# Expert steps of a diffusion trunk kernel: flips at the step's own end, small products placed among whole-array ones, the first light step one place earlier

## The chip, the cores and the metric

The kernel runs on one core of one Trainium2 chip. The metric is the time of one execution on the device in microseconds; three executions give 1393.93, 1398.74 and 1399.1 us, and their median is 1398.74 us. One more execution was taken with the hardware profiler.

## The reference

A trunk of two layers over 256 latent tokens of width 1024, with 256 context tokens beside them. Layer 0 is attention and a dense SwiGLU; layer 1 is a short convolution and then a top-2-of-8 expert SwiGLU, which is the part that the change touches:

```
logits = h @ router_w
top_vals, top_idx = top_k(logits, 2); gates = one_hot(top_idx) weighted by softmax(top_vals)
out = sum over e of gates[:, e] * swiglu(h, w_gate[e], w_up[e], w_down[e])
swiglu(h, g, u, d) = (silu(h @ g) * (h @ u)) @ d
x = x + g2 * out
```

All of it is float32. An expert's hidden width is 3584; the weights of the eight experts are 352 MB, and every one is read once.

## The kernel before, in words

**Steps.** The experts are ranked by how many tokens chose them (`ranks`). Rank 0 is expert 0 of the data; ranks 1 to 4 are heavy too and take up to 128 tokens, ranks 5 to 7 are light and take up to 64. Each expert is worked through in seven steps of 512 hidden columns, so there are 35 heavy and 21 light steps; `chunks` is their order. Heavy steps of rank 0 come first, then light ones are spread evenly among the heavy ones, and the last four are light. The first light step stands at place 5, counted from 0.

**One step** is a loop over p. In p = 0 to 7 TensorE makes gate and up for this step: a heavy step in 48 products of 128x128 by 512 columns, with each weight split into a high and a low part of float32r (`parts`: ScalarE makes `hi`, L74, VectorE `lo`, L75) and the tokens split likewise (`eh`, `el`); a light step in products of plain float32 with 64 columns of weights, gate and up side by side in the array (`pair`, L1340). In p = 8 to 11 it makes the down products of the step before (`down`), again split when that step was heavy, paired when it was light. Between them lie the activations: `hidden_part` makes silu(gate) * up in the tile `sg` (ScalarE L1333, VectorE L1334), of which there is one; `flip` transposes it in four blocks on TensorE (L1320); `turned` copies it out (ScalarE L1325 or L1328, VectorE L1329). Before the change `hidden_part` of a step is issued in its p = 9, and `flip` and `turned` in p = 3 and 4 of the next step. For a light step `flip` transposes 64 rows into 64 columns.

**Tasks.** Small pieces of work hang on hooks (step, p), run at the beginning of that p. For an expert whose first step is n and whose last is `end`: `choice` (one-hot of its tokens), `slots` (its transpose and the token list, on TensorE) with `slotted` (copies), `fetch_rows` (VectorE casts the list, POOL issues an indirect DMA that gathers the rows from `xd`, a copy of x in DRAM, L1253; the rows take one slot of the weights' ring), `scale_rows` (ScalarE, L1257), `turn_rows` (transposes, L1267) with `gathered` (ScalarE L1293 builds modulated rows in a tile `sg`, L1299 casts them into `eh`, VectorE L1300 makes `el`) or `gathered_light`; at the end `output` (VectorE L1350 into a tile `sg`, ScalarE L1352, VectorE L1353), `scatter` (TensorE, L1360) and `scattered` (VectorE, L1367).

**Order.** The order on each engine is the order in which the program issues, written out by hand. Weight loads of 1 MB are issued on SP's queue as slots of a ring of 13 come free; `ahead` issues the splits up to five halves before their use, into five buffers, and for a light step's weights, which TensorE reads unsplit, only the loads. A tile of a pool may be taken anew while an older use of it is still to be issued; the new writer then waits for the last reader. PSUM gives four tiles for products and transposes (`pm`) and four for the down sums (`acc`).

The main lines of the loop are L1455 to L1492, of the hooks L1369 to L1408, of `store_rows` L1442.

Of the kernel before, what the change touches and what calls it, by code (L numbers as in the profile page):

```python
# [8 lines left out]
F32 = mybir.dt.float32  # L9
F32R = mybir.dt.float32r  # L10
I32 = mybir.dt.int32
AF = mybir.ActivationFunctionType
# [4 lines left out]
KD = D // 128  # L17
S = 256
NT = S // 128
NE = 8  # L20
# [3 lines left out]
NL = 3  # L24
CAP = 64
# [8 lines left out]
def trunk(ctx, tc, i, out, dbg=None):  # L34
    nc = tc.nc
    pe, act, dve, sp = nc.tensor, nc.scalar, nc.vector, nc.sync
    dbg = dbg or {}

    def pool(name, bufs, space=None, side="left"):
        kw = {"space": space} if space else {"side": side}  # L40
        return tc.tile_pool(name=name, bufs=bufs, reuse_waits="tile", **kw)
# [7 lines left out]
    def acc():  # L49
        return cur["acc"].tile([128, 512], F32, name="acc")  # L50

    def pm():
        return cur["pm"].tile([128, 512], F32, name="pm")
# [25 lines left out]
    order = [i["w_out"][u] for u in range(4)]  # L79
# [7 lines left out]

    heavy = [(r, c) for r in range(NE - NL) for c in range(NFC)]
    light = [(r, c) for r in range(NE - NL, NE) for c in range(NFC)]
    mixed = [((2 * n + 1) / len(v), m, rc) for m, v in enumerate((heavy[4:], light[:-4])) for n, rc in enumerate(v)]  # L90
    chunks = heavy[:4] + [rc for *_, rc in sorted(mixed)] + light[-4:]
    who, whole = {}, []

    def weights(m, r, c, h):
# [45 lines left out]
    def ahead(split):  # L140

        n = used[0]
        step = 2 if whole[n // 2] else 1
        upto, k = n, n + step
        while split and k <= most[0] and k // 2 - n // 2 < 9:
            if whole[k // 2]:
                k += 2
            else:
                upto, k, split = k, k + 1, split - 1
        feed(upto)  # L150
        used[0] += step
        return ready.pop(n)
# [4 lines left out]
    x = const.tile([128, NT, D], F32, name="x")  # L157
    ident, sel = cid[:, 0:128], cid[:, 128:130]
# [482 lines left out]
    class Pair:  # L641
# [54 lines left out]
        def turned(self):  # L696
            self.pts = [pb2.tile([128, 512], F32, name="pt") for _ in range(2)]
            for e in range(2):
                act.copy(self.pts[e], self.tp[e])
# [31 lines left out]
    for n in range(NP + 3):  # L731
# [59 lines left out]
        if new is not None and n >= new + 2:  # L791
            a = n - new - 2
# [52 lines left out]
    class Boundary:  # L845
# [11 lines left out]
        def flip(self, t, g):  # L857
            for k in range(2):
                kk = 2 * g + k
                pe.transpose(self.turn[g][:, k, t * 128:(t + 1) * 128], self.xs[:, t, kk * 128:(kk + 1) * 128], ident)  # L860
# [122 lines left out]
    for g in range(NG):  # L983
# [10 lines left out]
        sg = ph.tile([128, 512], F32, name="sg")  # L994
        hd = ph.tile([128, 512], F32, name="hd")
# [37 lines left out]
    for j in range(4):  # L1033
# [9 lines left out]
        for m, ((_, p), (_, u)) in enumerate(zip(columns(pcc), columns(pu))):  # L1043
            n = m + 1 if j == 0 else 2
# [4 lines left out]
        for m in range(2):  # L1049
            k = 2 * j + m  # L1050
# [113 lines left out]
    me = ctx.enter_context(pool("me", 2))  # L1164
    xd = ctx.enter_context(tc.tile_pool(name="xd", bufs=1, space=bass.MemoryType.DRAM)).tile([S, D], F32, name="xd")

    gts = m1.tile([128, NT, NE], F32, name="gts")
    posr = m1.tile([128, NT, NE], F32, name="posr")
# [146 lines left out]

    def flip(C):
        C.ps = pm()
        w = CAP if C.E.light else 128
        for k in range(4):
            pe.transpose(C.ps[:, k * w:(k + 1) * w], C.hd[:, k * 128:(k + 1) * 128], ident[0:w, 0:w])  # L1320

    def turned(C):
        if C.E.light:
            C.dh = me.tile([128, 4 * CAP], F32, name="dT")
            act.copy(C.dh, C.ps[:, 0:4 * CAP])  # L1325
            return
        C.dh, C.dl = (me.tile([128, 512], F32R, name=n, bufs=1) for n in ("dh", "dl"))
        act.copy(C.dh, C.ps)  # L1328
        dve.tensor_sub(C.dl, C.ps, C.dh.bitcast(F32))  # L1329

    def hidden_part(C):
        sg = me.tile([128, 512], F32, name="sg", bufs=1)[0:CAP if C.E.light else 128]
        act.activation(sg, C.g, AF.Silu)  # L1333
        dve.tensor_mul(sg, C.u, sg)  # L1334
        C.hd = sg

    def pair(ps, lhsT, ws, first, last):

        for m, w in enumerate(ws):
            pe.matmul(ps[m * CAP:(m + 1) * CAP], lhsT, w, start=first, stop=last, tile_position=(0, m * CAP))  # L1340
# [25 lines left out]
        macc = cur["macc"]  # L1366
        dve.tensor_add(macc[:, t, c], (x if E is experts[0] else macc)[:, t, c], E.ps)  # L1367

    hooks = {}  # L1369

    def hook(n, p, f, *a):
        hooks.setdefault((n, p), []).append((f, a))

    def run(n, p):
        for f, a in hooks.pop((n, p), []):
            f(*a)

    experts = [Expert() for _ in range(NE)]
    for r, E in enumerate(experts):
        E.r, E.light = r, r >= NE - NL  # L1380
        E.ys, E.eh, E.el = [None, None], [None, None], [None, None]
        steps = [n for n, (v, _) in enumerate(chunks) if v == r]
        n, end = steps[0], steps[-1]
        if r:
            hook(n - 3, 10, choice, E, posr)
            hook(n - 2, 2, slots, E)
            hook(n - 2, 3, slotted, E)
            hook(n - 2, 4, fetch_rows, E)
            hook(n - 1, 2, scale_rows, E)
            if E.light:  # L1390
                hook(n - 1, 5, turn_rows, E, range(KD))
                hook(n - 1, 6, gathered_light, E)
            else:
                for g in range(2):
                    ks = range(4 * g, 4 * g + 4)
                    hook(n - 1, (5, 8)[g], turn_rows, E, ks)
                    hook(n - 1, (6, 9)[g], gathered, E, ks)
        else:
            hook(2, 1, choice, E, pos)
            hook(2, 2, slots, E)  # L1400
            hook(2, 3, slotted, E)
        if end < len(chunks) - 1:
            for q in range(1 if E.light else 2):
                hook(end + 2, (1, 4)[q], output, E, q)
            for m in range(4):
                q, t = (m % 2, m // 2) if E.light else (m // 2, m % 2)
                hook(end + 2 + m // 2, (6, 10)[m % 2], scatter, E, q, t)
                hook(end + 2 + m // 2, (8, 11)[m % 2], scattered, E, q, t)  # L1408
    choice(experts[0], pos, True)
    most[0] = 2 * len(order) - 1  # L1410
    feed(2 * FIRST + 3)
    for g in (0, 2):
        ks = [range(2 * g, 2 * g + 2), range(2 * g + 2, 2 * g + 4)]
# [13 lines left out]
    def down(C, s):  # L1427

        E, r = C.E, C.c * 4 + s
        if r == 0:  # L1430
            E.accs = [acc() for _ in range(1 if E.light else 2)]
        first, end = r == 0, r == 4 * NFC - 1
        if E.light:
            if s % 2 == 0:
                C.w = ahead(5)
            f = [slice(s % 2 * 1024 + 512 * q, s % 2 * 1024 + 512 * q + 512) for q in range(2)]
            pair(E.accs[0], C.dh[:, s * CAP:(s + 1) * CAP], [C.w[:, v] for v in f], first, end)
        else:
            k = slice(s * 128, (s + 1) * 128)
            mac(E.accs, C.dh[:, k], C.dl[:, k], *halves(ahead(4)), first, end)  # L1440

    def store_rows():  # L1442
        for t in range(NT):
            sp.dma_start(xd[t * 128:(t + 1) * 128, :], x[:, t])

    hook(0, 1, ranks)
    hook(1, 0, store_rows)
    hook(0, 3, by_rank, posr, pos)
    hook(1, 1, gates)
    hook(3, 2, gate_rows, 1, 5, (0, 1), g2)  # L1450
# [2 lines left out]
    last, final = None, len(chunks) - 1  # L1453
    for n, (r, c) in enumerate(chunks):
        E = experts[r]  # L1455
        C = Expert()
        C.E, C.c = E, c
        if E.light:
            C.gu = pm()
            C.g, C.u = C.gu[0:CAP], C.gu[CAP:]  # L1460
        else:
            C.g, C.u = pm(), pm()
        for p in range(8):
            run(n, p)
            if last and p == 3:
                flip(last)
            if last and p == 4:
                turned(last)
            if E.light:
                if p % 4 == 0:  # L1470
                    ws = [ahead(5) for _ in range(2)]
                f = slice(p % 4 * 512, p % 4 * 512 + 512)
                pair(C.gu, E.h[:, p], [w[:, f] for w in ws], p == 0, p == 7)
                continue
            half, m, j = p // 4, (p // 2) % 2, p % 2
            hi, lo = ahead(4)
            for k in range(2):
                f = slice(k * 512, (k + 1) * 512)
                kk = 4 * half + 2 * j + k
                mac([C.u if m else C.g], E.eh[kk // 4][:, kk % 4], E.el[kk // 4][:, kk % 4], [hi[:, f]], [lo[:, f]],  # L1480
                    kk == 0, kk == KD - 1)
        for p in range(8, 12):
            run(n, p)
            if p == (8 if n in (0, final) else 9):
                hidden_part(C)
            if n == final and p == 11:
                flip(C)
                turned(C)
            if last:
                down(last, p - 8)  # L1490
        last = C
    ends = {(q, t): pm() for q in range(2) for t in range(NT)}  # L1492

    macc = cur["macc"]
# [8 lines left out]
    for t in range(NT):  # L1503
        for q in range(2):
            c = slice(512 * q, 512 * q + 512)
# [159 lines left out]
```

## Time and profile before

| what | value |
|---|---|
| median of three executions | 1398.74 us |
| the profiled execution | 1398.09 us |
| its span | 1396.2 us |
| TensorE busy | 1359.2 us, 97% |
| VectorE busy | 987.4 us, 71% |
| ScalarE busy | 798.3 us, 57% |
| read from HBM | 470.21 MB, 338 GB/s over the span |

The span is the time between the first and the last instruction that the profile shows; the execution's own time is 1.9 us longer. TensorE is called PE, VectorE DVE, ScalarE ACT, GpSimd POOL and SyncE SP. A time such as 914.28 is counted in us from the start of the span. The expert stage begins at about 503 us. A duration of a product is that of one that fills and drains the array; the distance from one start to the next is what a product costs in a row of products. Fp32 products and transposes show as one or two records each.

### The profile page before, as it was taken

The page shows a single profiled execution, that of the slowest core. Times are in us where ns is not written, and L with a number is a line of the kernel's source. Part 1 is how long each engine was busy: PE and PEld are TensorE (multiplying, and loading weights), DVE is VectorE, ACT ScalarE, POOL GpSimd, SP SyncE. Part 2 cuts the span into 40 slices and gives each one's busy share as a digit, 9 for nine tenths or more (in the row PEclk, how much of TensorE's full clock was granted, in tenths as well). Part 3 has the DMA queues.
Part 4 walks back from the last instruction along what each step waited for, and adds up shares of the span by engine and source line. Part 5 has one row for each costly group of instructions (what it writes and reads, how often), then busy time and mean ns, then how long its engine had stood idle before and what let it go on. Part 6 is the DMA issues. An engine that isn't in the chain of part 4 may idle for free.

```text
span 1396.2 us, 20283 instructions
## 1 busy us (share of the span) xinstructions
PE 1359.2 (97%) x7596; PEld 997.2 (71%) x7596; DVE 987.4 (71%) x1338; ACT 798.3 (57%) x1077; POOL 10.3 (1%) x11
## 2 busy tenths in 40 slices
PE   6999999999999999999999999999999999999997
PEld 4776789999889977766666766657667666676742
DVE  5777769788778678866767667767577677676721
ACT  5567674444463377856656666656557566565610
POOL 0000000000000000000000000000000000000000
PEclk9999999999999999999999999999999999999999
DMA  9734678678767399798999999998999999999994
GB/s 376 278 121 141 253 301 302 241 284 295 266 240 255 144 377 357 262 422 333 420 421 421 419 377 420 407 400 367 419 414 421 415 383 379 405 421 418 415 419 165
DMA packets 67162, 473.71 MB, mean 339 GB/s; under 512 B 7472, under 2 KB 8112, under 8 KB 11120
## 3 DMA queue, kind: packets, MB, share of 16 engines
q1 hardware_dynamic: 66240, 469.46, 84.2%
q0 software_dynamic: 816, 2.88, 0.6%
q8 instruction: 61, 1.00, 0.3%
q14 instruction: 45, 0.37, 0.1%
HBM read 470.21 MB, written 2.10 MB: 338 GB/s over the span
## 4 chain that ended last, share of the span: by engine, by line
PE 88%; DVE 5%; ACT 4%; DMA 2%; issue 1%; SPq 0%; ACTq 0%; DVEq 0%
PE pm L1340 11%; PE pm L274 9%; PE pm L276 8%; PE pm L278 8%; PE acc L274 8%; PE acc L276 7%; PE acc L278 7%; PE acc L1340 4%; PE pm L930 4%; PE pm L931 4%; PE pm L932 4%; PE pm L1320 2%; DVE lo L75 2%; DMA raw<-in_moe_g_dram 1%; ACT hi L74 1%
## 5 line engine op out<-in xcount | busy, mean ns | idle before, releaser
L75 DVE TENSOR_TENSOR lo<-raw,hi 128x1024 fp32r<-128x1024 f32 x522 | 627.0, 1224 | 135.8 <-ACT hi L74 113.1
L74 ACT ACTIVATE hi<-raw 128x1024 fp32r<-128x1024 f32 x522 | 546.2, 1061 | 246.0 <-PE pm L278 107.5
L274 PE MATMUL pm<-hi,eh 128*128 128x512 f32 x560 | 226.0, 404 | 0.4 <-ACT g L260 0.2
L276 PE MATMUL pm<-lo,eh 128*128 128x512 f32 x560 | 220.3, 393 | 2.1 <-DVE lo L75 2.0
L278 PE MATMUL pm<-hi,el 128*128 128x512 f32 x560 | 219.6, 392 | 0.0
L1340 PE MATMUL pm<-raw,hl 128*64 128x512 f32 x672 | 155.4, 599 | 0.0
L930 PE MATMUL pm<-th,hi 128*128 128x256 f32 x480 | 135.4, 282 | 0.0
L931 PE MATMUL pm<-tl,hi 128*128 128x256 f32 x480 | 135.0, 281 | 0.0
L932 PE MATMUL pm<-th,lo 128*128 128x256 f32 x480 | 135.0, 281 | 0.0
L274 PEld LDWEIGHTS pm<-hi,eh 128*128 128x128 f32 x560 | 105.8, 189 | 33.9 <-issue 8.0
L276 PEld LDWEIGHTS pm<-lo,eh 128*128 128x128 f32 x560 | 106.0, 189 | 24.7 <-DVE lo L75 4.5
L278 PEld LDWEIGHTS pm<-hi,el 128*128 128x128 f32 x560 | 105.8, 189 | 22.8
L1340 PEld LDWEIGHTS pm<-raw,hl 128*64 128x64 f32 x672 | 44.1, 136 | 80.6 <-issue 77.9
L930 PEld LDWEIGHTS pm<-th,hi 128*128 128x128 f32 x480 | 91.2, 190 | 1.2 <-issue 0.8
L932 PEld LDWEIGHTS pm<-th,lo 128*128 128x128 f32 x480 | 91.5, 191 | 0.0
L931 PEld LDWEIGHTS pm<-tl,hi 128*128 128x128 f32 x480 | 90.9, 189 | 0.4
L274 PE MATMUL acc<-hi,dh 128*128 128x512 f32 x280 | 88.7, 398 | 0.0
L276 PE MATMUL acc<-lo,dh 128*128 128x512 f32 x280 | 86.5, 390 | 0.0
L278 PE MATMUL acc<-hi,dl 128*128 128x512 f32 x280 | 86.3, 389 | 0.0
L1334 DVE TENSOR_TENSOR sg<-pm,sg 128x512 f32<-128x512 f32 (+1 forms) x56 | 38.6, 690 | 64.6 <-ACT sg L1333 64.3
L1340 PE MATMUL acc<-raw,dT 128*64 128x512 f32 x336 | 78.1, 600 | 0.0
L1333 ACT ACTIVATE sg<-pm 128x512 f32<-128x512 f32 (+1 forms) x56 | 32.8, 585 | 69.5 <-PE pm L1340 66.4
(329 smaller groups left out, 1613.4 us busy)
## 6 DMA issues: line engine op xcount, KB each, us to landing
raw<-in_moe_d_dram SPq DMA_DIRECT2D x112, 1024.0 KB, 12.8
raw<-in_moe_g_dram SPq DMA_DIRECT2D x111, 1024.0 KB, 13.1
raw<-in_moe_u_dram SPq DMA_DIRECT2D x111, 1024.0 KB, 12.9
raw<-in_ada_w_dram SPq DMA_DIRECT2D x48, 1024.0 KB, 6.7
raw<-in_conv_i_dram SPq DMA_DIRECT2D x12, 1024.0 KB, 7.0
raw<-in_ffn_g_dram SPq DMA_DIRECT2D x11, 1024.0 KB, 6.3
raw<-in_ffn_u_dram SPq DMA_DIRECT2D x11, 1024.0 KB, 5.7
raw<-in_ffn_d_dram SPq DMA_DIRECT2D x11, 1024.0 KB, 5.0
```

Source lines behind the costliest of these rows:

```text
L74: act.activation(hi, r, AF.Copy)
L75: dve.tensor_sub(lo, r, hi.bitcast(F32))
L274: pe.matmul(p, hh, wh[j], start=first, stop=False)
L276: pe.matmul(p, hh, wl[j], start=False, stop=False)
L278: pe.matmul(p, hl, wh[j], start=False, stop=last)
L930: pe.matmul(d, hi[:, c], th[:, k], start=(k == 0), stop=False)
L931: pe.matmul(d, hi[:, c], tl[:, k], start=False, stop=False)
L932: pe.matmul(d, lo[:, c], th[:, k], start=False, stop=(k == KD - 1))
L1320: pe.transpose(C.ps[:, k * w:(k + 1) * w], C.hd[:, k * 128:(k + 1) * 128], ident[0:w, 0:w])
L1333: act.activation(sg, C.g, AF.Silu)
L1334: dve.tensor_mul(sg, C.u, sg)
L1340: pe.matmul(ps[m * CAP:(m + 1) * CAP], lhsT, w, start=first, stop=last, tile_position=(0, m * CAP))
```

## The change

- The order of the steps: three heavy steps come first in place of four, so the first light step stands at place 4.
- `hidden_part` is issued right after p = 7 of its own step, and `flip` after p = 11 of its own step; `turned` follows in p = 1 of the next step (after the last step, at once).
- `flip` always transposes 128 rows by 128 columns; of a light step `turned` copies the 64 columns that matter.
- `slots`, `turn_rows` and `scatter` become tasks of a step, ordered by kind (turns, slots, scatters) and put at places that depend on the step: in a light step at p = 8, 9, 10, 11, in a heavy one at p = 4, 7, 9, 10, 11, each with its copies one p later. For slots the step is n - 3 (before: n - 2).
- `choice` goes to step n - 4, `fetch_rows` from p = 4 to p = 8 of step n - 2, `scale_rows` from p = 2 to p = 3 of step n - 1.
- `store_rows`, the copy of x to `xd`, goes from SP's queue to ScalarE's, and to step 0.

```diff
-    mixed = [... for m, v in enumerate((heavy[4:], light[:-4])) for n, rc in enumerate(v)]
-    chunks = heavy[:4] + [rc for *_, rc in sorted(mixed)] + light[-4:]
+    mixed = [... for m, v in enumerate((heavy[3:], light[:-4])) for n, rc in enumerate(v)]
+    chunks = heavy[:3] + [rc for *_, rc in sorted(mixed)] + light[-4:]
...
     def flip(C):
         C.ps = pm()
-        w = CAP if C.E.light else 128
         for k in range(4):
-            pe.transpose(C.ps[:, k * w:(k + 1) * w], C.hd[:, k * 128:(k + 1) * 128], ident[0:w, 0:w])
+            pe.transpose(C.ps[:, k * 128:(k + 1) * 128], C.hd[:, k * 128:(k + 1) * 128], ident)
...
-    hooks = {}
+    hooks, tasks = {}, {}
+
+    def task(n, order, *a):
+        tasks.setdefault(n, []).append((order, *a))
...
         if r:
-            hook(n - 3, 10, choice, E, posr)
-            hook(n - 2, 2, slots, E)
-            hook(n - 2, 3, slotted, E)
-            hook(n - 2, 4, fetch_rows, E)
-            hook(n - 1, 2, scale_rows, E)
+            hook(max(n - 4, 0), 10, choice, E, posr)
+            task(max(n - 3, 1), 1, [(slots, E)], [(slotted, E)])
+            hook(n - 2, 8, fetch_rows, E)
+            hook(n - 1, 3, scale_rows, E)
             if E.light:
-                hook(n - 1, 5, turn_rows, E, range(KD))
-                hook(n - 1, 6, gathered_light, E)
+                task(n - 1, 0, [(turn_rows, E, range(KD))], [(gathered_light, E)])
             else:
                 for g in range(2):
                     ks = range(4 * g, 4 * g + 4)
-                    hook(n - 1, (5, 8)[g], turn_rows, E, ks)
-                    hook(n - 1, (6, 9)[g], gathered, E, ks)
+                    task(n - 1, 0, [(turn_rows, E, ks)], [(gathered, E, ks)])
         else:
             hook(2, 1, choice, E, pos)
-            hook(2, 2, slots, E)
-            hook(2, 3, slotted, E)
+            task(2, 1, [(slots, E)], [(slotted, E)])
...
-                hook(end + 2 + m // 2, (6, 10)[m % 2], scatter, E, q, t)
-                hook(end + 2 + m // 2, (8, 11)[m % 2], scattered, E, q, t)
+                task(end + 2 + m // 2, 2, [(scatter, E, q, t)], [(scattered, E, q, t)])
+
+    for n, v in tasks.items():
+        v.sort(key=lambda a: a[0])
+        places = [(p, p + 1) for p in range(8, 12)] if chunks[n][0] >= NE - NL else [(4, 5), (7, 8), (9, 10), (10, 11), (11, 12)]
+        for (_, pe_, other), (p, q) in zip(v, places):
+            for fa in pe_:
+                hook(n, p, *fa)
+            for fa in other:
+                hook(n, q, *fa)
...
-            sp.dma_start(xd[t * 128:(t + 1) * 128, :], x[:, t])
+            act.dma_start(xd[t * 128:(t + 1) * 128, :], x[:, t])
...
-    hook(1, 0, store_rows)
+    hook(0, 2, store_rows)
...
         for p in range(8):
             run(n, p)
-            if last and p == 3:
-                flip(last)
-            if last and p == 4:
+            if last and p == 1:
                 turned(last)
...
+        hidden_part(C)
         for p in range(8, 12):
             run(n, p)
-            if p == (8 if n in (0, final) else 9):
-                hidden_part(C)
-            if n == final and p == 11:
-                flip(C)
-                turned(C)
             if last:
                 down(last, p - 8)
+        flip(C)
+        run(n, 12)
         last = C
+    turned(last)
```

## Rows read from the trace of the kernel before

**Rows 1.** The page: busy time, share of the span and instructions of each engine.

```profile
PE 1359.2 (97%) x7596; PEld 997.2 (71%) x7596; DVE 987.4 (71%) x1338; ACT 798.3 (57%) x1077; POOL 10.3 (1%) x11
```

**Rows 2.** Timeline of PE, three steps: start, us, operation, count [idle before, releaser].

```profile
914.28 0.66 PE L1320 MATMUL pm<-cid,sg 128*128 128x128 f32 x4
914.87 2.79 PE L1340 MATMUL pm<-raw,hl 128*64 128x512 f32 x12
...
930.42 0.39 PE L278 MATMUL pm<-hi,el 128*128 128x512 f32 x1
930.74 0.46 PE L1320 MATMUL pm<-cid,sg 64*128 64x64 f32 x4
931.13 0.50 PE L274 MATMUL pm<-hi,eh 128*128 128x512 f32 x1
931.47 0.39 PE L276 MATMUL pm<-lo,eh 128*128 128x512 f32 x1
...
938.16 3.65 PE L1340 MATMUL acc<-raw,dT 128*64 128x512 f32 x16
...
945.96 0.60 PE L1320 MATMUL pm<-cid,sg 128*128 128x128 f32 x4
946.32 0.48 PE L274 MATMUL pm<-hi,eh 128*128 128x512 f32 x1
946.64 0.40 PE L276 MATMUL pm<-lo,eh 128*128 128x512 f32 x1
...
953.26 0.62 PE L274 MATMUL acc<-hi,dh 128*128 128x512 f32 x2
...
958.79 1.51 PE L1340 MATMUL pm<-raw,hl 128*64 128x512 f32 x6
```

**Rows 3.** PE's gaps; a wait of DVE; two windows (PEclk third from the end).

```profile
537.62 0.43 PE L1305 MATMUL pm<-cid,oh 128*128 128x128 f32 x2 [1.62 <-DVE oh L1245]
...
719.48 0.66 PE L1320 MATMUL pm<-cid,sg 128*128 128x128 f32 x4 [1.52 <-DVE sg L1334]
...
900.04 0.47 PE L1360 MATMUL pm<-yh,ohTl 64*128 64x512 f32 x1 [1.74 <-DVE dl L1329]
...
DVE sg L1350 <- PE pm L1320: 18.3, 7, 7.4
...
538.90:542.20 3.30, 3.30 (x12) 2.62 (x11) 1.45 (x2) 1.50 (x2) 0.00 (x0) 0.50 1.01 402
717.00:720.40 3.40, 1.88 (x12) 0.70 (x10) 2.27 (x3) 1.16 (x3) 0.00 (x0) 1.00 1.01 419
```

**Rows 4.** Timeline of PE and DVE where the first expert step ends.

```profile
514.67 0.39 PE L274 MATMUL pm<-hi,eh 128*128 128x512 f32 x1
...
517.81 0.69 DVE L1334 TENSOR_TENSOR sg<-pm,sg 128x512 f32<-128x512 f32 x1
```

**Rows 5.** Groups by line from 520 us on: busy us, mean ns | idle before, releasers.

```profile
L1333 ACT ACTIVATE sg<-pm 128x512 f32<-128x512 f32 (+1 forms) x55 | 32.2, 585 | 69.4 <-PE pm L1340 66.4 <-DVE el L1300 3.0
...
L1325 ACT COPY dT<-pm 128x256 f32<-128x256 f32 x21 | 7.5, 358 | 15.6 <-PE pm L1320 15.6
...
L1257 ACT ACTIVATE raw<-raw,gs 128x1024 f32<-128x1024 f32 x4 | 4.6, 1139 | 5.4 <-DMA raw<-xd,idx 5.4
```

**Rows 6.** The gathers: one cast and its POOL issue (timeline); all seven landings (by line).

```profile
879.02 0.15 DVE L1250 CAST idx<-gsl 128x1 int32<-128x1 f32 x1
...
879.90 0.91 POOL L1253 DMA_INDIRECT raw<-xd,idx  x1 [79.00 <-ACT hi L74]
...
DMA to landing us min/median/max: 4.9/8.4/11.2
```

**Rows 7.** Groups by line, as in rows 5: the modulated rows and their cast.

```profile
L1293 ACT ACTIVATE sg<-pm,ada,amod 128x128 f32<-128x128 f32 x32 | 12.0, 455 | 7.8 <-PE pm L1267 7.8
...
L1299 ACT CAST eh<-sg 128x512 fp32r<-128x512 f32 x8 | 5.0, 621 | 0.3
```

**Rows 8.** Waits of SP's queue: us in total, times, longest us.

```profile
SPq L67 <- PE pm L1267: 58.2, 5, 15.8
```

More of the change, by code (lines that the diff above doesn't have):

```diff
@@ L89, in trunk @@
     light = [(r, c) for r in range(NE - NL, NE) for c in range(NFC)]
-    mixed = [((2 * n + 1) / len(v), m, rc) for m, v in enumerate((heavy[4:], light[:-4])) for n, rc in enumerate(v)]
-    chunks = heavy[:4] + [rc for *_, rc in sorted(mixed)] + light[-4:]
+    mixed = [((2 * n + 1) / len(v), m, rc) for m, v in enumerate((heavy[3:], light[:-4])) for n, rc in enumerate(v)]
+    chunks = heavy[:3] + [rc for *_, rc in sorted(mixed)] + light[-4:]
     who, whole = {}, []
@@ L1324, in turned @@
             C.dh = me.tile([128, 4 * CAP], F32, name="dT")
-            act.copy(C.dh, C.ps[:, 0:4 * CAP])
+            act.copy(C.dh.rearrange("p (k c) -> p k c", c=CAP), C.ps.rearrange("p (k c) -> p k c", c=128)[:, :, 0:CAP])
             return
@@ L1331, in hidden_part @@
     def hidden_part(C):
[L1332 to L1335, printed above, removed]
+        C.hd = me.tile([128, 512], F32, name="sg", bufs=1)
+        hd = C.hd[0:CAP if C.E.light else 128]
+        act.activation(hd, C.g, AF.Silu)
+        dve.tensor_mul(hd, C.u, hd)
     def pair(ps, lhsT, ws, first, last):
@@ L1406, in trunk @@
                 q, t = (m % 2, m // 2) if E.light else (m // 2, m % 2)
-                hook(end + 2 + m // 2, (6, 10)[m % 2], scatter, E, q, t)
-                hook(end + 2 + m // 2, (8, 11)[m % 2], scattered, E, q, t)
+                task(end + 2 + m // 2, 2, [(scatter, E, q, t)], [(scattered, E, q, t)])
[7 more added lines that the diff above has]
+                hook(n, q, *fa)
+        assert len(v) <= len(places)
     choice(experts[0], pos, True)
```

## The prediction

> **What bounds the kernel now.** I read the page first: TensorE is busy 97% of the span [rows 1]. Then TensorE's timeline through one light and two heavy steps, for the pace and the price of what stands between the products [rows 2]: they follow each other without idle time, about 0.23 us apart, so in the expert stage each microsecond added to or taken from TensorE's queue is one of the run. Then the few places where TensorE did wait, and the granted clock after them [rows 3]; then the first expert step, the gathers and the long ScalarE passes, because the change moves these [rows 4 to 7]. SP's waits came last [rows 8].
>
> A step has 8 gate/up phases and 4 down phases; T is the end of the eighth. Four down phases take 5.53 us after a heavy step (953.26 to 958.79), so a heavy phase is 1.38 us; 16 records of a light step, which are four phases, take 3.65 us [rows 2].
>
> **Flips and tasks among whole-array products.** A heavy step's four transposes among a light step's pairs hold TensorE for 0.59 us (914.28 to 914.87). Among heavy products they take 0.36 us (945.96 to 946.32) and stretch the next interval from 0.23 to 0.32, so 0.45. A light step's 64-row transposes among heavy products take 0.39 us (930.74 to 931.13), come 0.09 late and stretch the next interval by 0.11: 0.59 [rows 2]. After the change both kinds stand at their own step's end as full transposes, which I price at 0.45: 18 heavy flips before light steps and 17 light flips before heavy ones save 0.14 us each, 4.9 us. By the list of hooks, seven scatters, three row turns and two slot transposes leave a pair stretch; at the same 0.14 that is 1.7 us. Ends: 3 us (where a step's end borders on pairs a switch remains) to 9 us. I take **-6.6**.
>
> **Waits that go.** Step 2's slots waited 1.62 us for VectorE's one-hot; two phases later it is ready. A flip waited 1.52 us for a late product of silu and up at 719.48. A scatter waited 1.74 us at 900.04: VectorE had stood still at `output` (L1350), whose tile is the one that the flip two phases later still reads, seven times for 18.3 us in all [rows 3]. With the flip a step earlier that tile is free. After the first and third gap the granted clock is 0.50, the lower of its two levels, for 3.4 us, which loses 1.7; after the second it stays at 1.00 (one window of each case stands). Together 4.9 + 3.4: **-8.3**, ends 3.3 (if the splits come late again) and 10.
>
> **Step 0.** It has no down products. Its flip now comes straight after gate/up, which end at about 514.67, where step 1's products begin; the tile to be transposed was done at 518.50 (517.81 + 0.69) [rows 4]. VectorE's work ahead of it is not moved. TensorE idles 3.8 us where it ran step 1, with 1.7 us of lower clock after it, as after the 1.62 us gap: **+5.5**; ends 2 and 6. At the other end of the kernel the last flip loses the down piece that hid its copy: 0.36 us [rows 5] and the hand-over, **+0.5**; ends 0 and 1.
>
> **The gather.** `fetch_rows` moves from phase 4 to phase 8 of the step before the last one, behind `hidden_part`; its row turn goes from phase 5 to phase 4 where the step before the expert is heavy, and stays late where it is light. After T: silu 0.59, the product 0.69 and hand-overs, 1.6 us in all [rows 4, 5]; the index cast and POOL's start 0.9 (879.02 to 879.90); the landing 8.4 (4.9 to 11.2); the scaling 1.14 [rows 5, 6]. The scaled rows are there at T + 12.0 (8.5 to 14.8). TensorE comes to the turn at T + 11.5 where the down products are heavy and the next step too (5.5 + 0.45 + four phases of 1.38: experts 1, 2 and 5), at T + 9.6 where they are light (3.65 in place of 5.5: experts 6 and 7), at T + 13.3 for expert 3 (eight light phases, 7.3, before the turn) and T + 11.4 for expert 4. It waits 3 x 0.5, 2 x 2.4, 0 and 0.6: **+6.9**; ends 0 and 25. What is queued behind the waiting ScalarE is the splits of four phases on, which have about that slack. Before, the fetch left four phases earlier, and ScalarE waited for it once, 5.4 us [rows 5].
>
> The Trainium skill, *DMA: Bandwidth & Descriptors*, section "Anatomy of one DMA — SWDGE (gpsimd) path", fits 2.0 us plus the bytes over 436 GB/s, which is 3.2 us for 512 KB: no gather here landed in under 4.9 us, beside a full SP queue. By the page the rows would be there at T + 6.8 and this term nothing.
>
> **The shared tile.** `gathered` builds the modulated rows in the same single tile as `hidden_part`. Before, both groups were through when `hidden_part` took it. For experts 3 and 4 the step before is light, and the groups now come in phases 9 and 10, behind `hidden_part`: ScalarE must wait until the flip at the step's end has read the tile, as L1350 waited before [rows 3]. Then four activations of 0.455 and a cast of 0.62, 2.4 us, make the first half of the expert's rows [rows 7], and VectorE's 0.69 the low part; the next step's first products need both, 2.7 us after they could start. The second group, 2.4 us more on ScalarE, stands ahead of the fourth split: about 1.2 us. Two experts, **+7.8**; ends 0 (if a reader issued later isn't waited for) and 12 (the following `output` and its scatter late as well). For experts 1 and 2 only the second group is behind, and the next step's first four splits were made earlier, as the down products are light: nothing, up to 1 each.
>
> **Clock after the new waits.** Four are of 2.4 us and more. Two of the three gaps of [rows 3] cost 1.7 us; I take two of four: **+3.4**, ends 0 and 10.
>
> **What costs nothing.** The expert rows' store leaves SP for ScalarE's queue: two issues, under 1 us, covered by ScalarE's idle time in step 0. SP had waited there, and its loads leave sooner, but the ring's 13 slots bound how far ahead they get. The first light step one place earlier, and a ring slot that the gather holds for less time (SP waited 58.2 us, in 5 places, for row turns [rows 8]), put loads further ahead; TensorE hardly waits for a load now, so this is cover against late splits, not time.
>
> **Sum.** The profiled execution took 1398.09 us (span 1396.2, 1.9 around it), 0.65 below the median of 1398.74. -6.6 - 8.3 + 5.5 + 0.5 + 6.9 + 7.8 + 3.4 = +9.2: **1407.3 us**. About 0.5%, 7 us, is what a measurement of this kernel can tell from no change.
>
> **Rivals.**
> A, the faster side: gather and shared tile are both hidden. What decides is the landing: up to T + 9.6 less the 3.6 around it, 6 us, nobody waits; and the later reader must not be waited for. Then 1398.1 - 6.6 - 8.3 + 6.0 = 1389.2. For it: one gather landed in 4.9 us, and the page's figure gives the same; against it the median of 8.4 and the waits of L1350. 0.24.
> B: the gather is hidden (splits further ahead thin SP's queue), the shared tile stays, one low-clock stretch with it: 1389.2 + 7.8 + 1.7 = 1398.7. 0.2.
> C: the gathers land like the slowest, 11.2 us: 18 us more waits, 1425. Little speaks for all seven. 0.08.
> D: the change doesn't do what it says, since switching merely moves to the steps' ends: the 6.6 isn't saved, 1413.9. 0.06.
>
> **How the numbers follow.** The forecast has 0.42, with 1400 to 1415 as its own range; of it 0.27 lies over 7 us slower and 0.15 within. Faster is A, 0.24; same is 0.15 + B, 0.35; slower 0.27 + C + D, 0.41. The range, 1386 to 1418, reaches from a little under A (the smaller waits of L1350, some 2 us, may go too) past D, and leaves out C and the outer ends.
>
> **What would show it.** Right: a TensorE gap of 3 to 4 us at the end of step 0, then clock 0.50; row turns that wait for ScalarE's scaling, most for experts 6 and 7; ScalarE activations of L1293 that wait for L1320's transposes before experts 3 and 4; light steps 0.2 to 0.3 us shorter. Wrong: gathers that land within 6 us of their issue, or L1293 running before the flip; then it is A or B. Late splits behind DMA landings would be a fifth case.

## The result, and the profile after

Six executions of the changed kernel have a median of 1416.44 us (1413.21 to 1418.65), six executions of the kernel before 1398.92 us (1393.93 to 1403.38): a ratio of 1.012, interval 1.010 to 1.014. The change makes the kernel 17.5 us slower where 1407.3 us was forecast, +9.2 on the profiled execution it started from and +8.6 on the median of 1398.74. The sign and the range held; the size did not. The profiled execution took 1418.65 us, its span 1416.8.

The page's busy line of the changed kernel answers to [rows 1]:

```profile
PE 1361.9 (96%) x7596; PEld 1011.4 (71%) x7596; DVE 987.8 (70%) x1338; ACT 796.9 (56%) x1077; POOL 9.1 (1%) x11
```

DVE and ACT have what they had. PE's work is about the same, so the time went into PE's idle places and its clock. Groups of PE by line, of the changed kernel from 498 us on (busy us, mean ns | idle before, releasers), show the idle places:

```profile
L274 PE MATMUL pm<-hi,eh 128*128 128x512 f32 x560 | 226.6, 405 | 4.8 <-ACT eh L1299 4.5 <-ACT hi L74 0.3
...
L276 PE MATMUL pm<-lo,eh 128*128 128x512 f32 x560 | 221.7, 396 | 1.3 <-DVE lo L75 1.2
...
L1319 PE MATMUL pm<-cid,sg 128*128 128x128 f32 x220 | 34.4, 279 | 7.9 <-DVE sg L1334 5.8 <-DVE idx L1250 2.1
L1359 PE MATMUL pm<-yh,ohT 128*128 128x512 f32 x20 | 8.6, 430 | 2.0 <-ACT yh L1351 2.0
L1359 PE MATMUL pm<-yl,ohT 128*128 128x512 f32 x20 | 8.1, 406 | 0.5 <-DVE yl L1352 0.5
L1267 PE MATMUL pm<-cid,raw 128*128 128x128 f32 (+1 forms) x56 | 7.7, 274 | 9.3 <-ACT raw L1257 9.3
```

Three families: row turns that wait for the scaled rows (L1267, 9.3 us); what stands behind the shared tile (the first products of experts 3 and 4, L274, late splits, L276, row sums, L1359: 8.2 us together); and flips that wait for the hidden part (L1319, 7.9 us, of which 3.7 at the end of step 0). In the whole expert stage PE's gaps over 0.15 us add up to 27.05 us, 8.72 before; stretches at the lower clock that begin in it hold 20.5 us, 6.8 before. The stage itself, from the first expert product to the last product of the program, in the kernel before and in the changed one (windows: us, busy PE, PEld, DVE, ACT, POOL, PEclk, DMA share, GB/s):

```profile
502.81:1388.15 885.34, 876.31 (x3941) 579.38 (x3939) 612.49 (x636) 528.39 (x614) 10.08 (x7) 1.00 0.96 391
```

```profile
508.01:1408.68 900.67, 873.54 (x3941) 589.43 (x3939) 612.88 (x636) 526.95 (x614) 8.90 (x7) 0.99 0.93 378
```

It is 15.3 us longer. The changed kernel's profile also enters the stage 5.2 us later; that is not the change, as with only the gather taken back (below) the stage begins at 502.62 us. The largest gaps, from the changed kernel's timeline of PE:

```profile
523.74 0.97 PE L1319 MATMUL pm<-cid,sg 128*128 128x128 f32 x4 [3.71 <-DVE sg L1334]
...
1002.84 0.50 PE L274 MATMUL pm<-hi,eh 128*128 128x512 f32 x1 [2.25 <-ACT eh L1299]
...
1024.67 0.66 PE L1319 MATMUL pm<-cid,sg 128*128 128x128 f32 x4 [2.09 <-DVE sg L1334]
...
1204.34 0.66 PE L1319 MATMUL pm<-cid,sg 128*128 128x128 f32 x4 [2.09 <-DVE idx L1250]
...
1215.03 1.12 PE L1267 MATMUL pm<-cid,raw 64*128 64x64 f32 x8 [4.56 <-ACT raw L1257]
```

The three gaps of [rows 3] are gone. Beside these losses the change gains. Three plain steps in a row, a light and two heavy ones, first in the kernel before, then in the changed one (windows as above):

```profile
1083.39:1096.73 13.34, 13.34 (x61) 7.15 (x61) 6.20 (x7) 5.43 (x6) 0.00 (x0) 1.00 1.00 405
1096.73:1111.90 15.17, 15.17 (x69) 10.13 (x67) 12.88 (x11) 10.33 (x11) 0.00 (x0) 1.00 1.01 421
1111.90:1128.93 17.03, 17.03 (x79) 13.83 (x77) 13.41 (x14) 12.57 (x13) 0.00 (x0) 1.00 1.01 421
```

```profile
1089.66:1102.62 12.96, 12.96 (x61) 7.11 (x61) 6.01 (x7) 5.13 (x7) 0.00 (x0) 1.00 1.00 411
1102.62:1117.69 15.07, 15.07 (x71) 10.38 (x70) 12.44 (x11) 10.03 (x11) 0.00 (x0) 1.00 1.01 421
1117.69:1134.66 16.97, 16.97 (x79) 13.91 (x77) 14.08 (x15) 12.98 (x14) 0.00 (x0) 1.00 1.01 420
```

PE is busy throughout in both, and the three steps take 45.00 in place of 45.54 us. So the trace shows a change that gains in nearly every step and loses more in a handful of places. Which part costs how much was then measured.

### The profile page after: what moved, and what is told of

Its sections match the earlier page's. It is cut to its first block, busy times and chain, and to the rows that moved or that the text cites. A ratio compares the mean times of both kernels' runs of the same rounds, so it can differ in the third digit from the quotient of the medians.

```text
span 1416.8 us, 20285 instructions
## 1 busy us (share of the span) xinstructions
PE 1361.9 (96%) x7596; PEld 1011.4 (71%) x7596; DVE 987.8 (70%) x1338; ACT 796.9 (56%) x1077; POOL 9.1 (1%) x11
## 5 line engine op out<-in xcount | busy, mean ns | idle before, releaser
L274 PE MATMUL pm<-hi,eh 128*128 128x512 f32 x560 | 226.6, 405 | 4.8 <-ACT eh L1299 4.5
L276 PE MATMUL pm<-lo,eh 128*128 128x512 f32 x560 | 221.7, 396 | 1.3 <-DVE lo L75 1.2
L1339 PE MATMUL pm<-raw,hl 128*64 128x512 f32 x672 | 148.8, 595 | 0.0
L274 PEld LDWEIGHTS pm<-hi,eh 128*128 128x128 f32 x560 | 107.2, 191 | 27.1 <-ACT eh L1299 5.0
L276 PEld LDWEIGHTS pm<-lo,eh 128*128 128x128 f32 x560 | 107.3, 192 | 24.2 <-DVE lo L75 3.2
L274 PE MATMUL acc<-hi,dh 128*128 128x512 f32 x280 | 89.0, 399 | 0.0
L276 PE MATMUL acc<-lo,dh 128*128 128x512 f32 x280 | 86.6, 390 | 0.0
```

The lines of the kernel that those rows point to most:

```text
L274: pe.matmul(p, hh, wh[j], start=first, stop=False)
L276: pe.matmul(p, hh, wl[j], start=False, stop=False)
```

## The experiments

The 95% intervals of the ratios reach 0.2 to 0.3% to each side, so a difference between the medians of two kernels is known to some 4 us. Where it matters, the length of the expert stage in the profiles stands beside it.

### Undoing one part of the change at a time

**A tile of their own for the modulated rows of experts 3 and 4.**

```diff
     def modulated_rows(E, ks, name="sg", vector=False):
-        h = me.tile([128, 512 if name == "sg" else 256], F32, name=name, bufs=1)[...]
+        p = cur["y"] if name == "yl" else me
+        h = p.tile([128, 256 if name == "oh" else 512], F32, name=name, bufs=2 if name == "yl" else 1)[...]
...
-        h = h or modulated_rows(E, ks)
+        h = h or modulated_rows(E, ks, "yl" if E.r in (3, 4) else "sg")
```

> The changed kernel, with the modulated rows of experts 3 and 4 in tiles of their own (the buffers of yl, which lie unused in those steps) in place of the tile that the hidden part takes. Theory: sharing that tile costs not only the late splits but all that stands behind them (the next expert's first products, its output and row sums, its flip): the gaps of the two experts read off the changed kernel's trace are 7.7 and 7.2 us, and two stretches of 3.4 us at half clock follow them, so the time falls by 13 to 19 us, to 1398 to 1404 us. Rival 1, the prediction's own figure for this term: it falls by 7.8 us, to about 1408.6. Rival 2, the turns stand too near the end of a light step in any tile: the gap before the first product of experts 3 and 4 stays near 2.5 us and the time falls by less than 3 us.

Measured: 1402.61 us, 1.002 of before (1.0001 to 1.004): 13.8 us less than the changed kernel. The theory's band holds it; the prediction's own 7.8 does not, nor does rival 2. In the changed kernel, the chain before expert 3's first product (timeline of all engines):

```profile
1000.00 0.60 PE L1319 MATMUL pm<-cid,sg 128*128 128x128 f32 x4
1000.63 1.51 ACT L1293 ACTIVATE sg<-pm,ada,amod 128x128 f32<-128x128 f32 x4 [6.61 <-PE pm L1319]
1002.17 0.62 ACT L1299 CAST eh<-sg 128x512 fp32r<-128x512 f32 x1
...
1002.84 0.50 PE L274 MATMUL pm<-hi,eh 128*128 128x512 f32 x1 [2.25 <-ACT eh L1299]
```

ScalarE stands still for 6.61 us until the flip has read the tile, and then makes the first half of the expert's rows in front of a waiting TensorE. With the tile of their own, the groups of PE by line are:

```profile
L274 PE MATMUL pm<-hi,eh 128*128 128x512 f32 x560 | 225.5, 403 | 0.0
...
L1320 PE MATMUL pm<-cid,sg 128*128 128x128 f32 x220 | 34.6, 280 | 7.5 <-DVE sg L1335 5.8 <-DVE idx L1250 1.7
L1360 PE MATMUL pm<-yh,ohT 128*128 128x512 f32 x20 | 8.4, 420 | 0.0
...
L1267 PE MATMUL pm<-cid,raw 128*128 128x128 f32 (+1 forms) x56 | 7.9, 281 | 10.4 <-ACT raw L1257 10.3
```

The waits of L274 and of the row sums are gone, those of the turns and the flips stand. The steps around experts 3 and 4 are 2.56, 3.87, 2.27 and 4.59 us shorter: 4.83 us in the two steps that end with the late first products, and 8.46 in the two behind them, the knock-on (splits queued behind the late rows, then the output's row sums). In the profiles the stage is 13.1 us shorter than the changed kernel's: 7.7 in gaps (27.05 to 19.34), 1.7 for one stretch of low clock fewer, and 3.7 in products that no longer stand apart. The theory's sum was right, but not its parts: it counted the flips' waits, which stayed, and two stretches of low clock, of which one stayed.

**The gather back to the fifth place.**

```diff
-            hook(n - 2, 8, fetch_rows, E)
-            hook(n - 1, 3, scale_rows, E)
+            hook(n - 2, 4, fetch_rows, E)
+            hook(n - 1, 2, scale_rows, E)
```

> The changed kernel, with each gather issued at the fifth place of its step (before: the ninth) and the scaling at the third place of the next, as in the kernel before. Theory: what the later gather costs is TensorE's waits at the turns (0.69, 0.45, 2.00, 1.63 and 4.59 us in the trace of the changed kernel, 9.4 us together, and low clock behind two of them), so the time falls by 8 to 13 us, to 1403 to 1408 us. Rival 1, these waits overlap with the shared tile's: those of experts 4 and 7 stay and the time falls by only 3 to 4 us. Rival 2, an earlier gather takes a staging buffer from the weight loads for longer: what is won at the turns is lost at loads that come late, and the time stays within 3 us.

Measured: 1401.88 us, 1.0013 of before (0.9996 to 1.003), 14.6 us less than the changed kernel and more than the theory's 13. ACT's waits for gathered rows (us in total, times, longest), in the changed kernel and then here, and the group of PE's row turns here:

```profile
ACT raw L1257 <- DMA raw<-xd,idx: 19.9, 6, 7.0
```

```profile
ACT raw L1257 <- DMA raw<-xd,idx: 0.8, 1, 0.8
```

```profile
L1267 PE MATMUL pm<-cid,raw 128*128 128x128 f32 (+1 forms) x56 | 7.0, 256 | 0.0
```

TensorE's waits at the turns are gone, 9.3 us, and so is the lower clock that went with those of experts 6 and 7. Two stretches of 3.4 us stand behind other gaps now, though, and one is gone there, so that four are left of the six. Gaps are 10.5 us less in all (27.05 to 16.54), and two stretches at half clock are 3.4; the sum is 13.9, and the stage in the profile is 13.8 us shorter. Nothing came back at the loads, and the waits of experts 4 and 7 did not stay, so both rivals fall.

**Step 0's flip back into step 1.**

```diff
+            if n == 1 and p == 3:
+                flip(last)
-            if last and p == 1:
+            if last and p == (4 if n == 1 else 1):
                 turned(last)
...
-        flip(C)
+        if n:
+            flip(C)
```

> The changed kernel, with the first step's activations turned in the second step at its fourth place, as in the kernel before. Theory: the wait at the end of step 0 (3.8 us) and the clock behind it (1.7 us) go: the time falls by 4 to 6 us, to 1410.5 to 1412.5 us. Rival: the wait only moves the weight loads' lead; without it the first steps run into loads that are not there, as the kernel before did at its step 2, and the time falls by less than 2 us.

Measured: 1409.64 us, 1.0075 of before (1.0047 to 1.0104), 6.8 us less than the changed kernel, above the theory's band by less than the noise. The kernel with three edits below has the same edit, and in its trace step 0 takes 11.85 us in place of 16.35 and the next step runs at full clock: 4.5 us and a stretch of low clock, 1.7, make 6.2.

**The stores back on SP's queue.**

```diff
-            act.dma_start(xd[t * 128:(t + 1) * 128, :], x[:, t])
+            sp.dma_start(xd[t * 128:(t + 1) * 128, :], x[:, t])
-    hook(0, 2, store_rows)
+    hook(1, 0, store_rows)
```

> The changed kernel, with the two stores of the rows back on SP's queue at the start of step 1. Theory: the store's place costs nothing (0 to 1.5 us either way); the 4.9 us by which the changed kernel's profile enters the expert stage later are two low stretches of the clock in the first 40 us (3.9 us) and 1 us of clock at 500, which this edit does not touch. Rival: moving the store off SP's queue lets weight loads start earlier and push back loads of the stage before, and costs the 4.9 us: the time falls by 4 to 5 us, to 1411.5 to 1412.5 us, and the profile enters the expert stage near 503 us again.

Measured: 1416.39 us, 1.012 of before (1.0089 to 1.015): no difference to the changed kernel. The store's place costs nothing, as the prediction had it. This run was needed because in the changed kernel's profile the first expert product starts at 508.01 us, not at 502.81, and nothing in the expert stage explains that. The first 40 us of the profiled executions do in part: before, changed, and changed with the stores on SP (PEclk third from the end):

```profile
0.00:40.00 40.00, 26.39 (x183) 17.83 (x183) 22.32 (x54) 23.92 (x52) 0.20 (x4) 1.00 0.96 373
```

```profile
0.00:40.00 40.00, 26.49 (x163) 17.38 (x164) 20.24 (x48) 22.42 (x48) 0.20 (x4) 0.91 0.90 353
```

```profile
0.00:40.00 40.00, 26.37 (x179) 18.13 (x180) 21.67 (x52) 23.21 (x50) 0.20 (x4) 1.00 0.94 371
```

The changed kernel's profile caught two stretches of low clock in the opening, and from there on was 3.9 us late; a stretch at 496.6 us that is 10.2 us long, for 6.8 before, comes on top. With the stores on SP the opening ran at 1.00 and the stage began at 504.45, and yet the median is the same.

### The parts together

**Three edits.** The diffs of the tile, the gather and step 0's flip, together, on the changed kernel.

> The changed kernel with all three edits: tiles of their own for the modulated rows of experts 3 and 4, the gathers at the fifth place, and step 0's activations turned in step 1. Theory, that these are three separate costs and what the change gains lies beside them: against the changed kernel the single runs were 14, 14.5 and 6.5 us faster, so this is 32 to 35 us faster, 1382 to 1386 us, 13 to 18 us below the kernel before. Rival: the gather's and the tile's waits of experts 3, 4 and 7 hide behind one another, so that the sum is some 8 us less, 1390 to 1394 us.

Measured: 1383.48 us, 0.9889 of before (0.9866 to 0.9912), 33.0 us below the changed kernel; the three single differences sum to 35.2. They are separate costs, and the rival of overlap falls. Two waits of any size are left, the flips of steps 31 and 42, in one group of PE:

```profile
L1320 PE MATMUL pm<-cid,sg 128*128 128x128 f32 x224 | 34.6, 277 | 3.8 <-DVE sg L1335 3.8
```

In the changed kernel, VectorE in step 42 shows why (timelines of PE, for the first down product, where gate and up of that step end, and of DVE):

```profile
1198.59 3.65 PE L1339 MATMUL acc<-raw,dT 128*64 128x512 f32 x16
...
1196.07 0.74 DVE L1349 SCALAR_TENSOR_TENSOR sg<-acc,gs,g 128x512 f32<-128x512 f32 x1
1197.49 0.69 DVE L1352 TENSOR_TENSOR yl<-sg,yh 128x512 fp32r<-128x512 f32 x1 [0.69 <-ACT yh L1351]
1198.46 1.23 DVE L75 TENSOR_TENSOR lo<-raw,hi 128x1024 fp32r<-128x1024 f32 x1 [0.27 <-DMA raw<-in_moe_g_dram]
1199.60 0.68 DVE L1366 TENSOR_TENSOR xhat<-xhat,pm 128x512 f32<-128x512 f32 x1
1200.20 3.49 DVE L75 TENSOR_TENSOR lo<-raw,hi 128x1024 fp32r<-128x1024 f32 x3
1203.61 0.68 DVE L1334 TENSOR_TENSOR sg<-pm,sg 128x512 f32<-128x512 f32 x1
1204.21 0.14 DVE L1250 CAST idx<-gsl 128x1 int32<-128x1 f32 x1
```

The hidden product is through at 1204.29, 5.7 us after gate and up, behind four splits and a row sum, and these came after an output; in most steps of the same trace it takes 1.7 to 2.0 us. The silu before it is late as well, behind four splits on ScalarE (timeline of ACT):

```profile
1197.37 3.90 ACT L74 ACTIVATE hi<-raw 128x1024 fp32r<-128x1024 f32 x4
1201.17 0.57 ACT L1333 ACTIVATE sg<-pm 128x512 f32<-128x512 f32 x1
```

The flip waits for the product at its own step's end, and the index cast of expert 7's gather, which now stands behind it, is as late.

**Five edits.** So two more flips were moved into the next step, and otherwise only the place of step 0's flip within p = 3 of step 1 differs:

```diff
+        turn = {1: 3, 32: 3, 43: 1}.get(n, 0)
         for p in range(8):
+            if turn and p == turn:
+                flip(last)
             run(n, p)
-            if n == 1 and p == 3:
-                flip(last)
-            if last and p == (4 if n == 1 else 1):
+            if last and p == turn + 1:
                 turned(last)
...
-        if n:
+        if n not in (0, 31, 42):
             flip(C)
```

> As the kernel with all three edits, and also the activations of steps 31 and 42 are turned in the step after them (32 at the fourth place, 43 at the second). Theory: what is left at the two ends of steps that also carry an output and row sums is a wait of 2.1 and 1.7 us for VectorE's product of the hidden part, with 1.7 us of clock behind each, so this is 5 to 8 us below the kernel with three edits, 1375 to 1380 us. Rival: VectorE is behind there by its queue, whatever TensorE does, and TensorE waits at the next thing that it makes (row sums, next splits): within 2 us of the kernel with three edits.

Measured: 1376.75 us, 0.9853 of before (0.9826 to 0.988), 6.7 us below the kernel with three edits, in the theory's band by the medians. This version beats both kernels, by 22.8 and by 39.7 us. Its page's busy line, and the group of its flips:

```profile
PE 1344.6 (98%) x7596; PEld 1001.7 (73%) x7596; DVE 985.7 (72%) x1338; ACT 795.1 (58%) x1077; POOL 8.6 (1%) x11
```

```profile
L1320 PE MATMUL pm<-cid,sg 128*128 128x128 f32 x224 | 34.6, 277 | 0.1
```

Its gaps add up to 2.48 us, and no stretch of low clock begins between its first expert product and the final drain. TensorE does not wait elsewhere instead, so the rival falls. The working behind the theory's band is not borne out in full, though. The expert stage with three edits, then with five:

```profile
508.19:1375.47 867.28, 861.29 (x3941) 583.83 (x3939) 611.22 (x636) 526.02 (x614) 8.80 (x7) 1.00 0.97 395
```

```profile
502.96:1367.12 864.16, 861.61 (x3941) 583.74 (x3939) 610.88 (x636) 525.54 (x614) 8.42 (x7) 1.00 0.97 396
```

With three edits no low clock stands behind the two waits, and the stage is 3.1 us shorter here, about the waits alone. That the rest of the 6.7 us belongs to this edit is not shown: it is within the noise of the medians.

### One part alone, in the kernel before

**The later gather alone.**

```diff
-            hook(n - 2, 4, fetch_rows, E)
-            hook(n - 1, 2, scale_rows, E)
+            hook(n - 2, 8, fetch_rows, E)
+            hook(n - 1, 3, scale_rows, E)
```

> The kernel before, with each gather issued at the ninth place of its step in place of the fifth and the scaling one place later, as the change has it, and nothing else. Theory: the later gather costs by itself what taking it back gained in the changed kernel, 9 to 15 us, so 1408 to 1415 us. Rival 1, the prediction's own figure for the gather: 6.9 us, about 1406. Rival 2: in the kernel before turns stand one place later and nothing is behind on VectorE, so that landings of 8 to 9 us are still hidden: within 3 us of the kernel before.

Measured: 1411.84 us, 1.0082 of before (1.0059 to 1.0105): 12.3 us slower from two moved lines. The turns' gaps are 2.48, 1.86, 1.67 and 3.58 us, in one group where the kernel before has 0.7 (before, then here):

```profile
L1267 PE MATMUL pm<-cid,raw 128*128 128x128 f32 (+1 forms) x56 | 7.3, 260 | 0.7 <-ACT raw L1257 0.7
```

```profile
L1267 PE MATMUL pm<-cid,raw 128*128 128x128 f32 (+1 forms) x56 | 7.7, 270 | 9.6 <-ACT raw L1257 9.6
```

Windows behind the first, second and fourth of them (PEclk third from the end):

```profile
647.20:651.00 3.80, 3.80 (x12) 1.25 (x13) 1.38 (x2) 2.37 (x6) 0.00 (x0) 0.55 0.59 244
821.20:825.00 3.80, 3.80 (x12) 1.17 (x12) 1.31 (x2) 2.12 (x5) 0.00 (x0) 0.55 0.00 0
...
1005.80:1009.40 3.60, 3.42 (x10) 1.49 (x12) 0.77 (x2) 2.72 (x7) 0.00 (x0) 0.53 1.02 432
```

Each gap is followed by some 3.4 us at 0.5, the lower of the two levels (the third by 6.8). So the price is some 40% clock: 8.9 us more at turns (9.6 - 0.7), 6.8 for four more stretches of 3.4 us, half lost, less 3.3 for two gaps of [rows 3] (1.74 and 1.52) that vanish: 12.4, where the expert stage of the profile is 12.0 us longer.

**The flips alone.**

```diff
-                    hook(n - 1, (5, 8)[g], turn_rows, E, ks)
-                    hook(n - 1, (6, 9)[g], gathered, E, ks)
+                    hook(n - 1, (4, 6)[g], turn_rows, E, ks)
+                    hook(n - 1, (5, 7)[g], gathered, E, ks)
...
+        hidden_part(C)
         for p in range(8, 12):
             run(n, p)
-            if p == (8 if n in (0, final) else 9):
-                hidden_part(C)
...
+        if n:
+            flip(C)
         last = C
+    turned(last)
```

`flip`, `turned` and `hidden_part` are those of the change, and step 0 is flipped in step 1.

> The kernel before with its old order of steps, its gathers, slots and row sums where they were, and only the activations turned at their own step's end among whole-array products (but step 0's in step 1, and the row turns of experts 1 to 4 one and two places earlier so that they end before the hidden part takes the tile). Theory: switching among the light steps' products costs time and goes with the flips: 8 to 12 us faster, 1387 to 1392 us. Rival, the prediction's case in which switching saves nothing: within 3 us of the kernel before.

Measured: 1389.73 us, 0.9931 of before (0.9908 to 0.9953): 9.8 us faster. The plain steps here take 12.96, 15.07 and 16.97 us, as in the changed kernel. The expert stage, which took 885.34 us before:

```profile
502.74:1375.13 872.39, 865.89 (x3941) 582.21 (x3939) 611.93 (x636) 527.13 (x614) 8.37 (x7) 1.00 0.97 397
```

It is 12.9 us shorter: 2.4 are gaps (8.72 to 6.30, with one of 3.26 at a flip at 714.41), 3.4 the two stretches of low clock, which are gone, and 7.1 products that follow one another more closely. So switching does save time, and the prediction's rival D falls; but 5.8 of the 12.9 are not switching.

## Why the prediction was right and wrong

**What failed.** The sizes of two cost terms failed, and one wait was put at nothing. The first failed step is the shared tile, put at +7.8 with ends of 0 and 12: it measured 13.8 by the medians and 13.1 in the profile's stage, of which 1.7 is a stretch of low clock that the sum had under another term. The two late first halves are there as worked out (2.7 us each forecast, 2.25 in the trace). What was too small is the knock-on, 1.2 us for each expert and a late output only as a bound: splits queued behind the late rows, then the row sums of the output, then a stretch of low clock, 8.5 us in the two steps behind. The second is the gather: +6.9 for waits that measured 9.3, and with the low clock that came with them 14.6 taken back in the changed kernel and 12.3 added alone. Its landing was right (8.6 us median, 7.4 to 9.4, against 8.4), and so were the waits of experts 1, 3 and 6 (0.54, 0.17, 1.97); those of experts 2 and 5 were smaller (0.29 and none, for 0.5 each). Those of experts 4 and 7 were larger (1.80 and 4.56 for 0.6 and 2.4). Expert 4's rows came 9.3 us after their issue (1161.89 to 1171.16), near the slowest. For expert 7 the step "After T: silu 0.59, the product 0.69 and hand-overs, 1.6 us in all" failed: in step 42 it took 5.7 us. The landings:

```profile
DMA to landing us min/median/max: 7.4/8.6/9.4
```

**What was not seen.** The flips of steps 31 and 42 wait 2.09 us each for a product as late as that, and the sum had nothing for them; taken away they gave 6.7 us by the medians, 3.1 in the stage. The prediction moved VectorE's wait at `output` away and asked who waits next only for scatters, not for the flip now standing at the end of the same step. Low clock: the prediction's terms amount to three stretches of 3.4 us in the changed kernel's stage (one behind step 0, two behind the new waits); the trace has six, each losing 1.7 us, where there were two before.

**What held.** Step 0: +5.5 forecast, 6.8 measured, the same within the noise; the gap is 3.71 us, with a clock stretch behind it. The stores on ScalarE's queue: nothing. VectorE's waits at `output` for a flip fell from 18.3 us in seven places to 6.1 in two. The tail's half microsecond: the wait for `dT` is 0.52. The direction, and the three kinds of waits named as signs: all are there; light steps are 0.38 us shorter (13.34 to 12.96), more than the 0.2 to 0.3 named. The estimate of 3.2 us for a gather of 512 KB by the fit in the Trainium skill (*DMA: Bandwidth & Descriptors*, "Anatomy of one DMA — SWDGE (gpsimd) path") is met by none of the seven landings, 7.4 us at the least. Of the rivals, A and B needed a hidden gather, C landings of 11.2 us where the slowest took 9.4. The new order by itself was not run.

**What was too small on the good side.** Switching and waits were to give 14.9 us; the kernel with five edits, which has all of the change's gains and nearly none of its costs, shows 22.8. In its profile the expert stage is 21.2 us shorter: 6.2 are gaps (8.72 to 2.48), 3.4 clock, and so 11.5 products that follow one another more closely, for the 6.6 forecast. I had priced a flip among pairs by its own 0.59 us. But the pairs behind it lose too: the 32 records of a light step's pairs take 7.09 us unbroken (changed kernel) and 7.24 around a flip, beside its 0.59 (kernel before). A light and a heavy step together save 0.48 us, not 0.28, and heavy steps alone another 0.06. The flips alone gave 7.1 of the 11.5; how the other 4.4 divide between the tasks that left the pairs and the new order was not measured.

**Balance.** Costs by single runs: 13.8 + 14.6 + 6.8 + 6.7 = 41.9; gains 22.8; 19.1 against 17.5 measured, which agrees within the noise. By the stages of the profiles the costs are 36.5 (900.67 - 864.16), the gains 21.2 (885.34 - 864.16); the 15.3 between them follow by construction, so the check of the single terms is that the three costs added up. The prediction had 24.1 of costs (5.5, 0.5, 6.9, 7.8, 3.4) and 14.9 of gains. Both sides were under, by the stages by some 12 and 6 us, and the forecast stayed in its range because the two errors partly cancelled. That is luck, not a sum that held.

## What to carry to other kernels

When work is moved later, price it by the busiest step that it will stand in, not by a quiet one: read the other engine's queue between its input and its use, as in a step with an output a hand-over of 1.6 us became one of 5.7. A tile with one buffer turns one late reader into a chain, so follow it to the second and third waiter before putting a number on it. A change that is slower can hold a good part: here five edits of a few lines each turned +17.5 us into -22.8.

## What the runs showed of the hardware that was not expected

A gap of TensorE of about 2 us is followed by a stretch at the lower clock in some places and not in others: 1.97 at 878.5 and 2.09 at 1024.67 in the changed kernel were, 2.25 at 1002.84 and 2.09 at 1204.34 were not; with three edits 2.10 at 1008.99 and 1.66 at 1178.11 were not either; alone, the gather's gaps of 1.67 to 3.58 all were. What decides it stays open. Such a stretch of 3.4 us loses about 1.7 us, nearly as much again as the gap itself. And the opening of the program has low stretches in some executions and none in others, whatever was changed in the expert stage: the first expert product starts at 502.62 us (gather early), 504.45 (stores on SP), 505.26 (gather late alone) and 508.19 (three edits), so a difference of 4 us between two single profiles says nothing about a change, unless both are counted from the first expert product on.
